# Staggered sets of K pairs with paced loads in an FFN's down product, one Strassen pair more in a convolution's input product, and last output tiles in token halves

## The chip, the cores and the metric

The kernel runs on one core of a Trainium2 chip. The core's TensorE (PE) multiplies, with a separate queue of weight loads (PEld); VectorE (DVE) and ScalarE (ACT) do everything between products; GpSimd (POOL) and SyncE (SP) here only issue transfers, which share 16 DMA engines. Measured is the device time of one execution, in microseconds.

## The reference

A decoder trunk over 1024 tokens of width 1024, in float32:

```
h = x
for i in (0, 1):              # two of each, DEPTH = 2: one convolution layer, one MLA layer
    h = h + short_conv(rms_norm(h), w_in, conv_w, w_out)   or   h + mla(rms_norm(h), ...)
    h = h + swiglu(rms_norm(h), w13, w2)
out = rms_norm(h)

short_conv: u = h @ w_in;  gate_b, gate_c, val = split(u, 3)
            z = gate_c * val;  conv = sum(conv_w[k] * z shifted by 2-k tokens)
            (gate_b * conv) @ w_out
swiglu:     g, u = split(h @ w13, 2);  (silu(g) * u) @ w2        # hidden width 2816
mla:        queries, keys and values from latents, causal softmax per head, then @ w_o
```

The two layers are the convolution layer (loop index 0) and the MLA layer (index 1), each followed by its own FFN.

## The kernel before, in words

**Arithmetic.** Activations are kept transposed: features on the 128 partitions, the 1024 tokens along the free dimension, in two halves T1 and T2 of 512 tokens. An fp32 product is made of three fp32r matmuls: each operand is split (`split`, L90) into a rounded high part (an ACT cast, L92) and a remainder (a DVE subtraction, L93), and high·high, high·low and low·high are accumulated. One matmul is a 128x128 weight block by 512 tokens.

**Two kinds of products.** `classic` (L206) makes two output tiles of 1024 tokens from all K blocks: eight block products per K pair, 96 matmuls for K = 1024. `pair` (L144) is a Strassen–Winograd product of 2x2 blocks (two K blocks by two output tiles by two token halves): seven block products per K pair, "1", "5", "6", "2", "7", "3", "4" in the order `SEQ`, 84 matmuls for K = 1024 (four pairs, so 12 matmuls in a product). Each product needs its own weight mix (DVE additions L155 to L165, then a split into `wo`), and its own token mix, an operand `x1`, `x5`, ... of the K pair. `blocks` (L187) evacuates products 1, 5 and 6 by an ACT copy to half tiles `z` (L194), and the others by a DVE addition. `drip` takes work of other parts (token mixes, gates, statistics) from a queue of closures after each product.

**Stages.** Transposes of x and its split; `conv_in` (`first_product`, L557: the first three output pairs, `CLASSIC = 3`, by `classic`, the others by `blocks`, since the token mixes of x, `mix_x` L570, have to be made first); `conv_out` by `classic` into `h` (L674); FFN 1: `up` (22 output pairs, `blocks`) makes silu(g)·u, the seven operands of each of the 11 pairs of hidden tiles (`operands`, L242) are stored to a DRAM tensor `md` (512 KB each, pair `KEPT = 4` stays on the chip), and `back` (the down product, L475) reads them; the MLA stages with `w_o`; FFN 2 alike; the last norm with transposes back.

**The down product.** `back` runs over `GROUPS` of 2, 3, 3 and 3 K pairs; within a group over four pairs of output tiles `mp`, and for each of them the seven products of that group (6 matmuls in a product with two K pairs, 9 with three), accumulated into `h` by DVE (L500). The operands of a group are 14 or 21 tiles `xm` of 512 KB from a pool of 41 slots; those of the next group are loaded by the POOL queue (`load`, L686, issued in `move`, L85) after each `mp`, `pace` at a time, and the rest after the last `mp`. A load waits until its slot is free. Weights come by SP's queue (L140), four transfers for each `mp`, of 192 KB with three pairs and 128 KB with two, into ten buffers `w`.

**What sets the order.** Each engine's stream is ordered by a scheduler that simulates the program, so the order on an engine is not that of the code alone. Stalls at a place come from the semaphores that the instructions wait for.

## Time and profile before

Median of three runs 2104.06 us (2101.93 to 2107.01). The profiled execution took 2109.98 us, its recorded span is 2108.0 us.

| | before |
|---|---|
| span of the profiled execution | 2108.0 us |
| PE busy | 2071.3 us, 9606 matmuls and transposes |
| DVE busy | 1624.9 us |
| ACT busy | 932.0 us |
| POOL busy (issuing transfers) | 230.5 us |
| bytes moved | 321.24 MB, mean 152 GB/s |
| granted TensorE clock, mean | 0.992 |

Busy times are sums over the span. PE is pipelined, and its ends are modelled: whether PE is fed is better read from the number of matmuls that start in a stretch, at the 227 ns from one start to the next that a fed stretch shows. GB/s is what all queues moved together. "issue to landing" of a transfer includes the time that it stands behind others.

### The profile page before, as it was taken

The page shows a single profiled execution, that of the slowest core. Times are in us where ns is not written, and L with a number is a line of the kernel's source. Part 1 is how long each engine was busy: PE and PEld are TensorE (multiplying, and loading weights), DVE is VectorE, ACT ScalarE, POOL GpSimd, SP SyncE. Part 2 cuts the span into 40 slices and gives each one's busy share as a digit, 9 for nine tenths or more (in the row PEclk, how much of TensorE's full clock was granted, in tenths as well). Part 3 has the DMA queues.
Part 4 walks back from the last instruction along what each step waited for, and adds up shares of the span by engine and source line. Part 5 has one row for each costly group of instructions (what it writes and reads, how often), then busy time and mean ns, then how long its engine had stood idle before and what let it go on. Part 6 is the DMA issues. An engine that isn't in the chain of part 4 may idle for free.

```text
span 2108.0 us, 27158 instructions
## 1 busy us (share of the span) xinstructions
PE 2071.3 (98%) x9606; PEld 1721.6 (82%) x9606; DVE 1624.9 (77%) x2662; ACT 932.0 (44%) x1697; POOL 230.5 (11%) x440
## 2 busy tenths in 40 slices
PE   8999999999999999999999999999999999999998
PEld 6878887888888887788888888887888888878786
DVE  5797757789988887689558877767888888876775
ACT  6633344444444443224445555455444444442235
POOL 1000100000101121110001011100010010121100
PEclk9999999999999999999999999999999999999998
DMA  6133462343544587764222124532454454686751
GB/s 248 35 97 119 141 214 91 120 147 123 185 140 156 174 302 262 258 226 133 85 69 66 38 66 122 178 101 62 140 170 148 133 173 144 216 280 203 268 185 80
DMA packets 263399, 321.24 MB, mean 152 GB/s; under 512 B 18959, under 2 KB 207568, under 8 KB 263264
## 3 DMA queue, kind: packets, MB, share of 16 engines
q0 software_dynamic: 57792, 201.46, 28.0%
q1 hardware_dynamic: 205472, 118.07, 19.0%
q8 instruction: 75, 1.23, 0.2%
q14 instruction: 60, 0.49, 0.1%
HBM read 206.22 MB, written 108.00 MB: 149 GB/s over the span
## 4 chain that ended last, share of the span: by engine, by line
PE 92%; DVE 3%; DMA 2%; ACT 1%; issue 1%; SPq 0%; POOL 0%; POOLq 0%; DVEq 0%; ACTq 0%
PE ps_z L180 37%; PE ps_y L180 27%; PE ps_c L225 7%; PE ps_s L948 4%; PE ps_pv L983 2%; PE ps_t L972 1%; PE ps_wo L105 1%; PE ps_wo L107 1%; PE ps_wo L109 1%; PE ps_l L109 1%; PE ps_l L105 1%; PE ps_l L107 1%; DMA w<-in_mla_ffn_w_dram 1%; PE ps_q L105 1%; PE ps_q L107 1%
## 5 line engine op out<-in xcount | busy, mean ns | idle before, releaser
L180 PE MATMUL ps_z<-x,wo 128*128 128x512 f32 x2532 | 609.9, 390 | 3.6 <-ACT z L194 2.8
L180 PEld LDWEIGHTS ps_z<-x,wo 128*128 128x128 f32 x2532 | 475.5, 188 | 104.7 <-ACT z L194 4.1
L180 PE MATMUL ps_y<-x,wo 128*128 128x512 f32 x1764 | 432.3, 389 | 1.2 <-DVE x L93 0.9
L180 PEld LDWEIGHTS ps_y<-x,wo 128*128 128x128 f32 x1764 | 330.6, 188 | 70.9 <-DVE x L93 1.8
L92 ACT CAST wo<-w 128x512 fp32r<-128x512 f32 (+2 forms) x423 | 238.6, 570 | 281.1 <-PE ps_y L180 110.5
L93 DVE TENSOR_TENSOR wo<-w,wo 128x512 fp32r<-128x512 f32 (+2 forms) x423 | 260.8, 623 | 62.2 <-ACT wo L92 61.4
L180 PE MATMUL ps_z<-xm,wo 128*128 128x512 f32 x960 | 241.9, 395 | 7.9 <-DVE h L500 5.9
L180 PEld LDWEIGHTS ps_z<-xm,wo 128*128 128x128 f32 x960 | 180.8, 190 | 50.5 <-DVE h L500 7.8
L92 ACT CAST wo<-sums 128x512 fp32r<-128x512 f32 (+2 forms) x172 | 98.3, 572 | 260.9 <-PE ps_y L180 101.7
L180 PE MATMUL ps_y<-xm,wo 128*128 128x512 f32 x720 | 182.6, 392 | 2.3 <-DVE h L500 2.3
L180 PEld LDWEIGHTS ps_y<-xm,wo 128*128 128x128 f32 x720 | 135.2, 189 | 31.8 <-DVE h L500 3.1
L85 POOL DMA_DIRECT2D md<-x x140 | 75.0, 536 | 738.1 <-DVE x L93 695.6
L194 ACT COPY z<-ps_z 128x512 f32<-128x512 f32 x106 | 62.0, 585 | 136.5 <-PE ps_z L180 136.4
L93 DVE TENSOR_TENSOR wo<-sums,wo 128x512 fp32r<-128x512 f32 (+2 forms) x172 | 107.4, 624 | 14.2 <-ACT wo L92 12.9
L500 DVE TENSOR_TENSOR h<-ps_z,h 128x512 f32<-128x512 f32 x104 | 71.5, 688 | 40.5 <-PE ps_z L180 39.6
L85 POOL DMA_DIRECT2D xm<-md x140 | 74.1, 536 | 260.1 <-PE ps_z L180 138.3
L93 DVE TENSOR_TENSOR x<-t,x 128x512 fp32r<-128x512 f32 x136 | 92.2, 686 | 5.7 <-ACT x L92 5.7
L234 DVE TENSOR_TENSOR a<-ps_y,z 128x512 f32<-128x512 f32 x88 | 60.7, 689 | 42.3 <-PE ps_y L180 42.1
L92 ACT CAST x<-t 128x512 fp32r<-128x512 f32 x136 | 82.4, 620 | 20.8 <-DVE t L249 20.2
L955 ACT ACTIVATE p<-ps_s,mx,qscale 128x128 f32<-128x128 f32 (+3 forms) x64 | 53.4, 835 | 70.7 <-DVE mx L954 66.7
L155 DVE TENSOR_TENSOR sums<-w,w 128x512 f32<-128x512 f32 (+2 forms) x85 | 53.3, 627 | 31.3 <-DMA w<-in_mla_ffn_w_dram 15.1
L500 DVE TENSOR_TENSOR h<-ps_y,h 128x512 f32<-128x512 f32 x88 | 60.4, 686 | 20.7 <-PE ps_y L180 20.5
(295 smaller groups left out, 3213.6 us busy)
## 6 DMA issues: line engine op xcount, KB each, us to landing
md<-x POOLq DMA_DIRECT2D x140, 512.0 KB, 3.5
xm<-md POOLq DMA_DIRECT2D x140, 512.0 KB, 8.1
w<-in_conv_ffn_w_dram SPq DMA_DIRECT2D x88, 256.0 KB, 2.9
w<-in_mla_ffn_w_dram SPq DMA_DIRECT2D x88, 256.0 KB, 3.0
w<-in_conv_w_in_dram SPq DMA_DIRECT2D x48, 256.0 KB, 3.1
hd<-h POOLq DMA_DIRECT2D x24, 512.0 KB, 3.5
w<-in_conv_ffn_w_dram SPq DMA_DIRECT2D x48, 192.0 KB, 4.7
w<-in_mla_ffn_w_dram SPq DMA_DIRECT2D x48, 192.0 KB, 4.4
```

Of the source, the lines that this page charges most:

```text
L85: nc.gpsimd.dma_start(dst, src)
L92: nc.scalar.copy(out=hi, in_=src)
L93: (eng or nc.vector).tensor_tensor(lo, src, hi.bitcast(F32), ALU.subtract)
L105: nc.tensor.matmul(ps[:, hs], lhsT=wh, rhs=xh(k)[:, hs], start=st, stop=False)
L107: nc.tensor.matmul(ps[:, hs], lhsT=wh, rhs=xl(k)[:, hs], start=False, stop=False)
L180: mm = lambda w_, x_, f: nc.tensor.matmul(b, lhsT=w_[:, m], rhs=x_, start=f, stop=True, skip_group_check=True)
L194: nc.scalar.copy(out=kept[name], in_=b)
L225: nc.tensor.matmul(ps[:, ts], lhsT=w_[:, m], rhs=X[i][f"b{kh}{th}"][:, q, :], start=st and j == 0, stop=en and j == 2)
L234: nc.vector.tensor_tensor(dst, ps, add, ALU.add)
L500: nc.vector.tensor_tensor(dst[name], b, dst[name], ALU.add)
L948: nc.tensor.matmul(ps[:, a:b], lhsT=q[:, qs], rhs=k[:, a:b], start=i == 0, stop=i == 4 and b < kw)
L955: nc.scalar.activation(p, ps[:, :kw], AF.Exp, bias=mx, scale=qscale[:, qb:qb + 1], accum_out=rsum)
```

## The change

1. **conv_in.** `CLASSIC` goes from 3 to 2: the third output pair is made by seven products in place of eight. So that its token mixes are there earlier, `mix_x` and the statistics of x are started behind the first half of the first classic pair (hook `ahead`), and dripped in the numbers of `MIX`. The eight full-width ACT scalings of `xs` (`gains`, L580) go: the mixes take the gain in the DVE operation itself (`scalar_tensor_tensor`), and four half-width ACT scalings are left. The first Strassen pair takes its products in the order `SEQX`, "1", "2", "5", "6", "7", "3", "4", the three that need no mix being 1, 2 and 3. Product 7 of conv_in has its sign turned in both factors.
2. **down.** `GROUPS` becomes `SETS`, eight sets that are used by two `mp` each: `mp` 0 and 1 take (0, 10), (1, 2, 3), (4, 5, 6), (7, 8, 9); `mp` 2 and 3 take (0, 1), (2, 3, 4), (5, 6, 7), (8, 9, 10). A set has two or three pairs, as before, and the number of matmuls is the same. Pair 3 is kept on the chip, pair 10's operands are made first in `up`, and pair 10 is loaded twice: 77 loads in place of 70 for each FFN. A load of `xm` is issued behind the evacuation of a certain product (a dependency that POOL waits for): one load for each 1.5 products for the first 14, then one for 4/3 products. The 14 loads of the first set go one behind each evacuated product of the last two `up` output pairs, what is left of them right after. In the first sets the weight splits are ordered behind the evacuation four products back (`behind`), and the drip is thinner.
3. **conv_out and w_o.** The last output tile is made T2 first, then T1. The operands of the last K pair for the FFN are made in three steps: 1 and 5 before, 6, 3 and 7 behind T2, 2 and 4 behind T1; the statistics of the last four tiles come after that.
4. **Half tiles.** Six shared buffers become three for `z` and three for the rest.

The diff, cut to its core:

```diff
-CLASSIC = 3
+CLASSIC = 2
+MIX = ((3, 4), (5, 4))
-GROUPS = ((0, 1), (2, 3, 4), (5, 6, 7), (8, 9, 10))
-KEPT = 4
+LATE = 4
+SETS = ((0, 10), (0, 1), (1, 2, 3), (2, 3, 4), (4, 5, 6), (5, 6, 7), (7, 8, 9), (8, 9, 10))
+KEPT = 3
+AHEAD = 4
+PACE = (1.5, 10, 4 / 3)
...
     def half(name, dt=F32):
-        return slots.tile([P, HS], dt, name=name, tag="half", bufs=NHALF)
+        kind = "z" if name[0] == "z" else "half"
+        return slots.tile([P, HS], dt, name=name, tag=kind, bufs=NHALF // 2)
...
+    def behind(n):
+        with ExitStack() as stack:
+            seen = set()
+            for inst in reversed(marks[:max(0, len(marks) - n + 1)][-4:]):
+                if inst is not None and inst.ins.engine not in seen:
+                    seen.add(inst.ins.engine)
+                    stack.enter_context(tc.issue_after(inst.ins))
+            yield
...
-            split(hi, lo, source(name))
+            with behind(ahead):
+                split(hi, lo, source(name))
...
-            hook(name, b)
-            drip(1 if len(queue) < 14 else 2)
+            marks.append(hook(name, b))
+            if paced and marks[-1] is not None:
+                paced.popleft()(marks[-1])
+            if name in thin:
+                drip(1 if len(queue) < 14 else 2)
...
+            split_t = late and mi == 2
+            for ths in (((2, T2),), ((1, T1),)) if split_t else (((1, T1), (2, T2)),):
...
+                if split_t:
+                    emit(mi, ps, ths[0][1])
...
-    def back(w, load, st, final, ready, kept):
+    def back(w, load, st, final, ready):
...
+        todo = []
+        for q in range(1, len(SETS)):
+            new = [k for k in SETS[q] if k != KEPT and k not in SETS[q - 1]]
+            todo += [(kp, name) for name in SEQ for kp in new]
+        nload, products = len(todo), [0]
+        def pace(i):
+            return PACE[0] * i if i < 14 else PACE[1] + PACE[2] * i
+        for t in range(2 * len(SETS)):
+            mp, kps = t % (KD // 2), SETS[t // 2]
...
+            def hook(name, b):
...
+                while todo and pace(nload - len(todo)) <= products[0]:
+                    kp, nm = todo.pop(0)
+                    ready.setdefault(kp, {})[nm] = load(kp, nm, done)
+                products[0] += 1
+                return done
...
+            pair(w2, kps, [ready[kp] for kp in kps], n1 * P, n2 * P, hook, thin=("1", "5", "6") if t == 0 else SEQ[::2] if first else SEQ, ahead=AHEAD if first else 99)
...
+        def last(step):
+            mp = KD // 2 - 1
+            n = 2 * mp + (step > 1)
+            if step == 1:
+                fin["x"] = [slot("xg"), slot("xg")]
+                scaled(fin["x"][0], n)
+                X.append({})
+                fin["put"] = operands(*fin["x"], X[mp].__setitem__, "15")
+            else:
+                scaled(fin["x"][1], n, T2 if step == 2 else T1)
+                fin["put"]("637" if step == 2 else "24")
+                drip()
...
+            def ahead(mi):
+                with ExitStack() as behind:
+                    for inst in ready:
+                        behind.enter_context(tc.issue_after(inst.ins))
+                    if run["n"] == 0 and mi == 1:
+                        x_stats()
+                        mix_x()
+                    drip(MIX[run["n"]][mi - 1])
...
-            def mixed(name, x, y, o=o, t=t):
+            def mixed(name, x, g, y, o=o, t=t):
                 t[name] = half("t" + name)
-                tt(t[name], x, t[y] if isinstance(y, str) else y, ALU.subtract)
+                stt(t[name], x, g, t[y], ALU.mult, ALU.subtract)
                 o[name] = op_split("x" + name, t[name])
...
-        def load(kp, name):
+        def load(kp, name, behind=None):
             o = slot("xm", F32R, [P, 2, HS])
-            move(o, md[kp, SEQ.index(name)])
+            d = move(o, md[kp, SEQ.index(name)])
+            if behind is not None:
+                tc.add_manual_dep(d.ins, behind.ins.name, SYNC)
...
-        order = [k for kp in range(KF // 2) if kp != KEPT for k in (2 * kp, 2 * kp + 1)] + [2 * KEPT, 2 * KEPT + 1]
+        kpo = [SETS[0][1]] + [kp for kp in range(KF // 2) if kp not in (KEPT, SETS[0][1])] + [KEPT]
+        order = [k for kp in kpo for k in (2 * kp, 2 * kp + 1)]
...
-            if j == order[-3]:
-                for name in SEQ:
-                    ready[0][name] = load(GROUPS[0][0], name)
-        for name in SEQ:
-            for i, kp in enumerate(GROUPS[0]):
-                if i:
-                    ready[i][name] = load(kp, name)
+            if j in order[-3:-1]:
+                kp = SETS[0][j == order[-2]]
+                for name in SEQ:
+                    paced.append(lambda done, kp=kp, name=name: ready[kp].__setitem__(name, load(kp, name, done)))
```

`project_o` makes its last tile in token halves in the same way as `classic`.

**POOL, end of `up` and start of the down product of FFN 1.** A row is a transfer; brackets hold what it waits for: PE_, DVE_ and Activation_ are those engines' progress, DMASW and DMAHW earlier transfers. Before, the loads of the first group's second pair and of the next group:

```order
L85 DMA md<-x_6136 128x1024 [waits DMASW5_49,DVE_49]
L85 DMA trig<-cos 128x1024 [waits DMASW6_49,Activation_49]
L85 DMA md<-x_6160 128x1024 [waits DMASW7_49,DVE_49]
L85 DMA xm<-md 128x1024 [waits DMASW3_49,DMASW0_49,PE_49]
L85 DMA xm<-md 128x1024 [waits DMASW1_49,PE_49]
L85 DMA xm<-md 128x1024 [waits DMASW2_49,PE_49]
L85 DMA xm<-md 128x1024 [waits DMASW4_49]
L85 DMA xm<-md 128x1024 [waits DMAHW0_49,PE_49]
```

and with the change:

```order
L89 DMA md<-x_6085 128x1024 [waits DMASW2_49,DVE_49]
L89 DMA md<-x_6106 128x1024 [waits DMASW3_49,DVE_49]
L89 DMA xm<-md 128x1024 [waits Activation_49]
L89 DMA xm<-md 128x1024 [waits DMASW6_49,DMASW5_49,Activation_49]
...
L89 DMA md<-x_6142 128x1024 [waits DMASW7_49,DVE_49]
L89 DMA trig<-cos 128x1024 [waits DMASW0_49,Activation_49]
L89 DMA md<-x_6168 128x1024 [waits DMASW1_49,DVE_49]
L89 DMA xm<-md 128x1024 [waits DMASW2_49,DVE_49]
L89 DMA xm<-md 128x1024 [waits DMASW3_49,DVE_49]
```

Before, a load waits for PE, which has to be done with what was in its slot; with the change it waits for the ACT copy or the DVE addition of a product, and the stores to `md` stand between the loads.

**PE, start of conv_in.** `ps_c` is a classic tile, `rp` spreads the statistics, `ps_z` and `ps_y` are Strassen products. Before:

```order
L374 MATMUL vps<-ident,vrows 128x77
L225 MATMUL ps_c<-xb,wc 128x512 x286
L334 MATMUL rp<-identr,rh 128x128
L334 MATMUL rp<-identr,rl 128x128
...
L180 MATMUL ps_z<-xb,wo_839 128x512 x12
L180 MATMUL ps_y<-x_528,wo_858 128x512 x3
L180 MATMUL ps_y<-x_607,wo_858 128x512 x3
```

and with the change:

```order
L252 MATMUL ps_c<-xb,wc 128x512 x142
L364 MATMUL rp<-identr,rh 128x128 x2
L203 MATMUL ps_z<-xb,wo_711 128x512 x12
L364 MATMUL rp<-identr,rl 128x128
...
L203 MATMUL ps_z<-x_406,wo_768 128x512 x2
L252 MATMUL ps_c<-xb,wc 128x512 x48
L203 MATMUL ps_y<-xb,wo_730 128x512 x12
L203 MATMUL ps_z<-x_406,wo_768 128x512
L203 MATMUL ps_z<-x_429,wo_768 128x512 x3
```

The three classic pairs (288 matmuls) are two (192), and product 1 and the start of product 6 of the first Strassen pair stand ahead of the last 48 classic matmuls.

**PE, from conv_out to FFN 1.** `yop` and `yb` are operands of conv_out, `x_...` those of the FFN. Before, behind the last classic matmul:

```order
L225 MATMUL ps_c<-yb_2141,wc 128x512
L180 MATMUL ps_z<-x_2348,wo_2819 128x512 x3
...
L180 MATMUL ps_y<-x_2682,wo_2839 128x512 x3
L180 MATMUL ps_z<-x_2776,wo_2819 128x512
L180 MATMUL ps_y<-x_2781,wo_2839 128x512
...
L180 MATMUL ps_z<-x_2358,wo_2860 128x512 x3
```

and with the change:

```order
L252 MATMUL ps_c<-yop,wc 128x512 x18
L252 MATMUL ps_c<-yb_2142,wc 128x512 x3
L252 MATMUL ps_c<-yb_2145,wc 128x512 x3
L203 MATMUL ps_z<-x_2352,wo_2819 128x512 x3
...
L203 MATMUL ps_y<-x_2690,wo_2839 128x512 x3
L252 MATMUL ps_c<-yop,wc 128x512 x18
L252 MATMUL ps_c<-yb_2136,wc 128x512 x3
L252 MATMUL ps_c<-yb_2139,wc 128x512 x3
L203 MATMUL ps_z<-x_2749,wo_2819 128x512
L203 MATMUL ps_y<-x_2754,wo_2839 128x512
...
L203 MATMUL ps_z<-x_2362,wo_2860 128x512 x3
```

The 18 matmuls of products 1 and 5 with the first three K pairs stand between the two token halves of the last tile, and those with the last K pair follow the T1 half.

254 lines of the change are left out of this document (135 added, 119 removed).

## Prediction

> **What bounds the kernel now.** I read the page first (busy times and the chain of waits by engine), then PE's waits, then the stretches around each wait, then what else ran there.
>
> ```profile
> PE 2071.3 (98%) x9606; PEld 1721.6 (82%) x9606; DVE 1624.9 (77%) x2662; ACT 932.0 (44%) x1697; POOL 230.5 (11%) x440
> PE 92%; DVE 3%; DMA 2%; ACT 1%; issue 1%; SPq 0%; POOL 0%; POOLq 0%; DVEq 0%; ACTq 0%
> 339.79 12.48 PE ps_c L225 x55
> ```
>
> PE is the bound. A piece of the chain without a wait (third row) gives 12.48/55 = 0.227 us for a matmul; this is the price of every matmul below. An edit can gain only by fewer matmuls or by filling PE's gaps, which are few:
>
> ```profile
> PE ps_z L180 <- DVE h L500: 5.9, 2, 3.0
> PE ps_z L180 <- ACT z L194: 2.8, 3, 1.2
> PE ps_y L180 <- DVE h L500: 2.3, 2, 2.0
> PE ps_z L180 <- DVE wo L93: 1.3, 2, 0.8
> PE ps_z L180 <- ACT wo L92: 1.3, 2, 1.1
> PE ps_y L180 <- DVE x L93: 0.9, 2, 0.5
> ```
>
> (Total us, times, longest.) What a gap costs is read from the stretch around it, as its length less its matmuls at 0.227. Columns: length, PE busy, PEld, DVE, ACT, POOL, clock, DMA share, GB/s; the rows are start of down 1, two thirds into its group of pairs 2 to 4, start of down 2, the same place in down 2, conv_out to FFN 1, w_o to FFN 2.
>
> ```profile
> 786.00:796.00 10.00, 8.22 (x33) 5.84 (x33) 8.77 (x20) 5.39 (x13) 1.58 (x3) 1.00 1.13 395
> 868.00:878.00 10.00, 7.11 (x25) 5.40 (x24) 4.30 (x9) 1.48 (x3) 3.10 (x6) 0.83 1.13 395
> 1866.00:1878.00 12.00, 9.76 (x35) 7.27 (x34) 9.86 (x20) 5.42 (x13) 2.64 (x5) 0.86 1.13 391
> 1953.00:1963.00 10.00, 7.02 (x24) 5.35 (x23) 4.64 (x9) 1.54 (x3) 2.96 (x6) 0.83 1.13 394
> 352.00:362.00 10.00, 8.34 (x36) 6.03 (x35) 9.36 (x15) 9.07 (x15) 0.53 (x1) 1.00 0.36 105
> 1435.00:1447.00 12.00, 10.34 (x43) 7.67 (x43) 11.50 (x17) 10.21 (x17) 0.53 (x1) 1.00 0.32 88
> ```
>
> Lost: 10 - 33 x 0.227 = 2.5 us; 4.3; 4.1; 4.6; and from the busy time 1.66 at each of the last two. Single matmul records can be missing, so each is good to some 0.3. The three rows with a clock of 0.83 to 0.86 lose about 1.7 us to it (0.17 x 10): the waits of 2.0 to 3.0 us also halved the clock for a while, which those of up to 1.2 us did not.
>
> The Trainium skill, page "TensorE: Matmul & The Clock Gate", section "Part 1: The HAM clock gate (the "warmup" mystery)", has the clock halve after an idle window of about 3.4 us. Here 2.0 us was enough, so the trace decides. By the page's figure those three places would cost their waits alone, 7.9 us, and the sum below would be -11.8 in place of -16.9.
>
> Why the three are late stands in the chain, and in what POOL did just before:
>
> ```profile
> 863.88 8.48 DMA w<-in_conv_ffn_w_dram
> 1861.50 7.87 DMA w<-in_mla_ffn_w_dram
> 1948.74 8.58 DMA w<-in_mla_ffn_w_dram
> 859.11 1.19 POOL L85 DMA_DIRECT2D xm<-md  x2 [34.24 <-PE ps_z L180]
> 870.66 0.53 POOL L85 DMA_DIRECT2D xm<-md  x1 [0.15 <-issue]
> 873.70 2.49 PE L180 MATMUL ps_z<-xm,wo 128*128 128x512 f32 x6 [2.89 <-DVE h L500]
> xm<-md POOLq DMA_DIRECT2D x140, 512.0 KB, 8.1
> w<-in_conv_ffn_w_dram SPq DMA_DIRECT2D x88, 256.0 KB, 2.9
> w<-in_conv_ffn_w_dram SPq DMA_DIRECT2D x48, 192.0 KB, 4.7
> ```
>
> POOL waits 34 us for slots and then issues 12 loads between the fourth and fifth of these rows: 12 x 524 KB at the 395 GB/s of the window row are 16 us of transfers. A weight load of 192 KB that falls among them takes 8.48 us, where 256 KB in `up` take 2.9. The DVE sum that needs the weights stands ahead of the DVE addition to `h` that PE waits for. Without the 2.89 us the load could have taken 5.6.
>
> **The change part by part.** Durations are from the one profiled execution (2109.98 us, span 2108.0); it is 5.9 us above the median of the runs, 2104.06, and I apply the sum to the median.
>
> *Down, steady.* The matmuls are the same. Seven loads more for each FFN are 14 x 0.53 us of POOL issue and 14 x 1.3 us of transfer (524 KB at 395 GB/s); POOL is 11% busy, so neither lies on PE's path. What matters is the pace. With three pairs a product is 9 x 0.227 = 2.04 us, a load for 4/3 products is 193 GB/s, and the weights (4 x 197 KB for seven products) 55: 248. With two pairs, 1.36 us and 1.5 products: 257 + 55 = 312. Both are below 395, and a weight load finds at most one or two `xm` loads ahead of it: 2.9 us (as in `up`) and 1.3 for one give 4.2, under 5.6. In the changed order a load of `xm` stands 64 and more matmuls (14.5 us) ahead of its first use, after the first set, against a landing of 8.1. So I take the three stalls as gone: -(4.3 + 4.1 + 4.6) = -13.0. Bounds: 0 (all stay) and -13.0. If a load gets late after all, its product is what PE waits for, at a price like those three rows, 4.3.
>
> *Down, start.* The two-pair products are short for DVE:
>
> ```profile
> L93 DVE TENSOR_TENSOR wo<-w,wo 128x256 fp32r<-128x256 f32 x18 | 7.3, 420 | 4.7 <-ACT wo L92 4.7
> L500 DVE TENSOR_TENSOR h<-ps_z,h 128x512 f32<-128x512 f32 x46 | 31.6, 688 | 16.3 <-PE ps_z L180 15.8
> L93 DVE TENSOR_TENSOR x<-t,x 128x512 fp32r<-128x512 f32 x4 | 2.7, 686 | 0.0
> 778.55 9.70 DMA xm<-md
> ```
>
> A product of 1.36 us asks 0.42 of split, up to 0.42 of weight sum and 0.69 of accumulation, 1.1 to 1.5, while the operands of the last hidden pair (0.69 of split, and a mix and a cast) are still in the queue: hence DVE's 8.77 of 10 in the first window row, and 2.5 us lost. The change drips these operands at fewer products and sets the splits four evacuations back, but the DVE work is the same. I take half, -1.2; bounds 0 and -2.5. At the seam the loads are closer than elsewhere: the order has the tightest 38 matmuls (8.6 us) ahead of its use, and eight loads, two stores and `trig` within 62 matmuls (14.1 us): 5.8 MB, 409 GB/s against the 395 seen, 0.5 us over. POOL waits at each paced load for a product; behind it stand stores of the last pair to `md`, whose slots nobody needs within those 14 us. At the nearest rows a late load costs between 0.5 and 4.3 for each FFN; I take nothing, as half of the gap at the start is left in the sum.
>
> *conv_in.* One pair has 12 matmuls fewer: -2.7. The waits at the first Strassen pair, and the work that moves forward:
>
> ```profile
> 118.22 2.56 PE L180 MATMUL ps_z<-x,wo 128*128 128x512 f32 x10 [0.83 <-DVE wo L93]
> 123.48 2.79 PE L180 MATMUL ps_z<-x,wo 128*128 128x512 f32 x11 [0.44 <-ACT z L194]
> 24.50:90.20 65.70, 65.70 (x284) 54.27 (x285) 35.92 (x63) 42.95 (x112) 0.53 (x1) 0.98 0.26 88
> L580 ACT ACTIVATE xs<-xs,vec x8: 1157/1160/1166, 25.8 to 40.7; 128x1024 f32<-128x1024 f32 x8
> L406 ACT ACTIVATE sq<-xt 128x256 f32<-128x256 f32 x32 | 12.8, 412 | 0.0
> L92 ACT CAST x<-t 128x512 fp32r<-128x512 f32 x16 | 8.8, 632 | 0.0
> L93 DVE TENSOR_TENSOR x<-t,x 128x512 fp32r<-128x512 f32 x16 | 10.5, 686 | 2.0 <-ACT x L92 2.0
> ```
>
> The cover shrinks from 284 classic matmuls (65.7 us) to 192 (43.6). ACT had 42.95 in the longer stretch; it loses 8 x 1.16 and gains four half-width scalings (0.63 each, as a cast), so 36 us have to go into 43.6, with DVE's mixes (16 x (0.69 + 0.69) = 22) behind them in turn. Walking the changed order with these durations I find ACT late by about 1.5 us where product 6 waits for its cast and the next classic tile for its copies, and by 0.6 us at product 5: 2.1 in place of today's 0.83 + 0.44 = 1.3. Net -2.7 + 0.8 = -1.9. Bounds: -4.0 (no wait left), and +1.9 if these waits merge into one that halves the clock (4.6, as in the fourth window row).
>
> *conv_out and w_o.*
>
> ```profile
> 354.61 3.73 ACT x L92 x7
> 357.90 0.73 PE L180 MATMUL ps_y<-x,wo 128*128 128x512 f32 x2 [0.47 <-DVE x L93]
> 359.82 2.56 PE L180 MATMUL ps_z<-x,wo 128*128 128x512 f32 x10 [1.19 <-ACT z L194]
> ```
>
> Today the last tile's seven casts fill ACT, and the `z` copy that product 6 needs stands behind them. With halves, x1 and x5 are ready behind the T1 matmuls, so 0.47 goes; the `z` copies then stand behind the T1 scaling (0.63, as a cast of this width) and a square, and I expect two waits of some 0.6 us: 1.2 in place of 1.66 at each of the two, -0.4 each, -0.8 together. Bounds 0 and -3.3. The half pool gives `z` three buffers for three tiles at a time, and moves nothing.
>
> Sum: -13.0 - 1.2 - 1.9 - 0.8 = -16.9. The profiled execution would be 2093.1, the median 2087.2. As runs shorter than the profiled one may have shorter late loads to win back, I round up: **2088**.
>
> **Rivals.**
>
> *The loads collide at the seam.* Against it speaks 409 to 395 GB/s, a small excess; for it, that DVE is full there (8.77 of 10), so a late load finds no slack. If each start of down keeps or makes a stall of 4.3 us, 2 x 4.3 = 8.6 come back: 2096.
>
> The Trainium skill, page "DMA: Bandwidth & Descriptors", section "Specifications", gives about 358 GB/s as the limit of HBM for a core; by that the 14.1 us at the seam would be 16.1, which is this rival. The trace has 395 GB/s over 10 us, so I give the page's figure little weight.
>
> *Nothing is gained beyond conv_in.* Twelve loads in a row are gone, but DVE does the same work in down (77% busy over the span), and a mean pace of 312 GB/s with bunching in POOL's queue could make 4 us stalls elsewhere. Three stalls of 4.3 us that only change place leave -1.9 - 0.8 = -2.7 or, with conv_in at its worse bound, about +1: 2101 to 2105, around 2102.
>
> *Slower: paced loads late in the two-pair sets.* If a load takes the 9.70 us of the start of down rather than 8.6, each of seven products waits 1.1 us, and as its evacuation releases the next load, the lateness is handed on. With the clock halved meanwhile (7 x 1.36 more), 7.7 + 9.5 = 17.2 for each FFN, 34 for both, against -16.9: 2121. It decides from a landing of 8.6 us on, at one load for each product. Against it: 9.70 was measured among some ten loads in a row, and only three of the loads have less than 11 us.
>
> **How the numbers follow.** Forecast (2080 to 2095) 0.62; seam 0.16; no gain 0.13; slower 0.09. Low end: all bounds together, -13.0 - 2.5 - 4.0 - 3.3 = -22.8, would be 2081; with a run's spread, 2080. High end: the seam with a poor conv_in, 2101. A measurement here can tell about 0.2%, 4.2 us, from no change: faster than 2099.9 has 0.62 + 0.16, within it 0.13, slower 0.09.
>
> **What would show it.** In the changed profile, the chain has no weight load of 8 us in the down products, and no stretch of 10 us there has a clock below 0.95; PE's waits for DVE `h` fall from 8.2 us to under 2; the loads of `xm` land in under 8.1 us, spread evenly; conv_in has a wait of 1 to 2 us around 60 to 65 us, and the start of FFN 1 one of about 0.6 twice. Wrong would be: a wait for `xm` in the first set; a halved clock in conv_in; weight loads of 192 KB still at 4.7 us.

## The result, and the profile after

The change took 2114.14 us (median of six runs, 2107.26 to 2116.11) against 2106.65 us for the kernel before (six runs, 2101.93 to 2109.38). The ratio is 1.0039, 95% interval 1.0027 to 1.0052: slower, by more than a measurement can tell from no change, and above the upper end of the range. The profiled execution of the change took 2113.69 us, its span 2111.9, 3.9 us above the span before. The profiled execution of the kernel before (2109.98 us) is slower than any of its six runs here, so the two profiles show about half of the 7.5 us between the medians.

From the page of the changed kernel, busy times of the engines and two kinds of transfers (size, median us from issue to landing):

```profile
PE 2069.0 (98%) x9594; PEld 1719.5 (81%) x9594; DVE 1629.7 (77%) x2674; ACT 927.9 (44%) x1698; POOL 237.6 (11%) x454
xm<-md POOLq DMA_DIRECT2D x154, 512.0 KB, 5.1
w<-in_conv_ffn_w_dram SPq DMA_DIRECT2D x48, 192.0 KB, 4.2
```

The 12 matmuls are gone, and the loads of `xm` land in 5.1 us where they took 8.1. The weight loads of `down` are at 4.2 us in the median where they were at 4.7. By medians the change did what it says. PE's waits of the changed kernel (total us, times, longest) say something else:

```profile
PE ps_z L203 <- DVE h L533: 16.9, 9, 4.0
PE ps_z L203 <- ACT z L220: 1.4, 2, 0.8
PE ps_c L252 <- ACT v L265: 0.8, 1, 0.8
```

L533 is the old L500, the addition of a product to `h`; before, PE waited for it four times, 8.2 us in all. Now it does so nine times, and no row of the view names `xm`. The chain of waits of the changed kernel (start, length, what) has behind these stalls weight loads, and loads of `hs`, the residual, which `back` adds to `h` in the third quarter of `down` (L549, the old L513):

```profile
873.44 7.18 DMA w<-in_conv_ffn_w_dram
889.60 6.52 DMA w<-in_conv_ffn_w_dram
...
937.05 7.65 DMA hs<-hd
...
946.68 3.80 PE ps_z L203 x9
...
955.80 7.72 DMA w<-in_conv_ffn_w_dram
```

The loads are no longer than the worst of before (8.48 and 8.58 us), but there are more of them that somebody waits for. After the stall the nine matmuls at 946.68 take 3.80 us, 0.42 each: the halved clock again. What is late at 873.44 is seen on DVE. From the timeline of DVE in the changed kernel (start, busy, instruction, in brackets the idle time before it and its releaser):

```profile
872.86 0.55 DVE L99 TENSOR_TENSOR wo<-w,wo 128x384 fp32r<-128x384 f32 x1
...
876.63 1.02 DVE L99 TENSOR_TENSOR wo<-w,wo 128x384 fp32r<-128x384 f32 x2
880.74 0.56 DVE L176 TENSOR_TENSOR sums<-w,w 128x384 f32<-128x384 f32 x1 [3.10 <-DMA w<-in_conv_ffn_w_dram]
881.22 0.68 DVE L533 TENSOR_TENSOR h<-ps_z,h 128x512 f32<-128x512 f32 x1
```

The split at 872.86 frees a buffer, and the weight load starts at 873.44 (the chain). DVE comes to the sum that reads these weights (L176) at 880.74 - 3.10 = 877.64, 4.2 us behind the start of the load, and waits 3.10 us for the rest of its 7.18. The addition L533, for which PE waits, comes behind this sum in DVE's stream and is held up with it. PE then stands for 1.59 us:

```profile
881.96 3.92 PE L203 MATMUL ps_z<-xm,wo 128*128 128x512 f32 x16 [1.59 <-DVE h L533]
```

Nobody needs this sum soon: it belongs to the pair of output tiles after next, some 22 us further on. The kernel before has such a sum at the same place:

```profile
872.48 0.56 DVE L155 TENSOR_TENSOR sums<-w,w 128x384 f32<-128x384 f32 x1 [4.39 <-DMA w<-in_conv_ffn_w_dram]
```

DVE came to it at 872.48 - 4.39 = 868.09, also 4.2 us behind the start of its load (863.88, of 8.48 us). So this distance is not new.

The waits view groups DVE's waits for transfers in `down` of FFN 1 (785 to 1000 us), first of before, then of the change:

```profile
DVE sums L155 <- DMA w<-in_conv_ffn_w_dram: 9.6, 6, 4.4
DVE h L513 <- DMA hs<-hd: 0.5, 1, 0.5
```

```profile
DVE sums L176 <- DMA w<-in_conv_ffn_w_dram: 10.6, 4, 4.2
DVE h L549 <- DMA hs<-hd: 7.8, 5, 5.2
```

The waits for weights are about the same; those for `hs` are new. The tile view of `hs` has the eight loads and the eight additions of this FFN (durations in ns, first and last start in us), first before, then the change:

```profile
L512 SPq DMA_DIRECT2D hs<-hd x8: 338/339/362, 876.2 to 931.6; - x8
L513 DVE TENSOR_TENSOR h<-h,hs x8: 1218/1220/1227, 897.4 to 944.3; 128x1024 f32<-128x1024 f32 x8
```

```profile
L548 SPq DMA_DIRECT2D hs<-hd x8: 339/366/436, 890.1 to 937.5; - x8
L549 DVE TENSOR_TENSOR h<-h,hs x8: 1217/1226/1226, 898.2 to 947.4; 128x1024 f32<-128x1024 f32 x8
```

Load by load, DVE came to these additions 4.9 to 30.3 us behind the start of the load before, and 2.6 to 9.4 us with the change. The loads took 3.7 to 12.2 us before and 5.0 to 9.8 with the change: they are not slower, their readers are closer.

What this costs PE is seen over the same 215 us (length, busy times with counts, clock, DMA share, GB/s; matmuls are counted in the first bracket), first before, then the change:

```profile
785.00:1000.00 215.00, 210.12 (x911) 171.28 (x910) 169.48 (x297) 72.27 (x137) 28.55 (x54) 0.99 0.68 225
```

```profile
785.00:1000.00 215.00, 202.41 (x867) 163.89 (x866) 160.99 (x283) 71.11 (x137) 34.45 (x66) 0.98 0.76 236
```

At 0.227 us a matmul that is 8.2 us lost before and 18.2 with the change. The table below does the same sum by parts of the program for each profiled execution: over all matmuls, the time from one start to the next beyond what a fed stretch shows, in us. Its first columns answer to the parts of the prediction; "seams" are conv_out to FFN 1 and w_o to FFN 2. `down` ends with its last matmul; the waits of the last norm are under "other". Each part is good to some tenths, `up` comes out slightly below nothing, and each row is one execution of its kernel. The experiments in it follow below.

```
                           conv_in  seams  up 1+2  down 1  down 2  other  total
before                         1.5    5.0    -0.6     8.7    10.9   22.9   48.4
the change                     2.1    2.9    -0.5    18.1     9.1   23.3   54.9
change, old down               2.1    3.0     8.2     8.3    11.1   23.7   56.2
before, new down               1.5    4.9    -0.5    17.4    10.0   23.7   57.1
change, all splits 4 back      2.1    2.8    -0.6     4.5     2.2   23.7   34.8
before, splits 4 back          1.5    6.6    -0.5    10.5     9.7   24.1   51.7
change, splits 12 back         2.1    2.9    -0.6     9.6     9.0   25.0   47.9
change, 4 back, not paced      2.1    2.8    -0.6     4.9     1.3   23.2   33.7
change, old down, 4 back       3.0    3.0     6.2    11.3     9.0   22.0   54.5
change, loads not paced        2.9    2.8    -0.6     6.9     8.7   21.3   42.0
before, new down, 4 back       1.5    6.5    -0.6     5.9     2.5   21.6   37.5
change, 12 back, hs too        2.1    2.9    -0.6     4.9     3.7   23.7   36.6
change, hs ordered             2.1    2.8    -0.6     8.3    13.3   24.0   49.8
change, few xm loads           2.1    2.9    -0.7     1.8     1.9   22.8   30.8
```

Between the first two rows lies 54.9 - 48.4 = 6.5, and with 12 matmuls fewer (2.7) 3.8 us, the 3.9 us between the spans. Nearly all of the loss is in `down`, 27.2 in place of 19.6, and there in that of FFN 1 (18.1 for 8.7), while that of FFN 2 lost 1.8 less. There the additions of `hs` wait 0.7 us in all, in FFN 1 7.8.

### The profile page after: what moved, and what is told of

Its sections match the earlier page's. It is cut to its first block, busy times and chain, and to the rows that moved or that the text cites. A ratio compares the mean times of both kernels' runs of the same rounds, so it can differ in the third digit from the quotient of the medians.

```text
span 2111.9 us, 27202 instructions
## 1 busy us (share of the span) xinstructions
PE 2069.0 (98%) x9594; PEld 1719.5 (81%) x9594; DVE 1629.7 (77%) x2674; ACT 927.9 (44%) x1698; POOL 237.6 (11%) x454
## 4 chain that ended last, share of the span: by engine, by line
PE 88%; DVE 5%; DMA 4%; issue 2%; ACT 1%; POOL 0%; SPq 0%; POOLq 0%; DVEq 0%; ACTq 0%
PE ps_z L203 35%; PE ps_y L203 26%; PE ps_c L252 6%; PE ps_s L1019 4%; PE ps_pv L1054 2%; PE ps_t L1043 1%; DMA w<-in_conv_ffn_w_dram 1%; PE ps_wo L112 1%; PE ps_wo L114 1%; PE ps_wo L116 1%; DMA w<-in_mla_ffn_w_dram 1%; PE ps_l L116 1%; PE ps_l L112 1%; PE ps_l L114 1%; DVE h L533 1%
## 5 line engine op out<-in xcount | busy, mean ns | idle before, releaser
L203 PE MATMUL ps_z<-x,wo 128*128 128x512 f32 x2568 | 616.8, 389 | 1.7 <-ACT z L220 1.4
L203 PEld LDWEIGHTS ps_z<-x,wo 128*128 128x128 f32 x2568 | 481.6, 188 | 103.5 <-ACT z L220 3.2
L203 PE MATMUL ps_z<-xm,wo 128*128 128x512 f32 x960 | 245.9, 398 | 17.7 <-DVE h L533 16.9
L203 PEld LDWEIGHTS ps_z<-xm,wo 128*128 128x128 f32 x960 | 181.6, 191 | 62.6 <-DVE h L533 18.2
L89 POOL DMA_DIRECT2D xm<-md x154 | 81.5, 531 | 377.3 <-DVE h L533 256.9
L533 DVE TENSOR_TENSOR h<-ps_z,h 128x512 f32<-128x512 f32 x104 | 71.3, 688 | 42.6 <-PE ps_z L203 42.5
L176 DVE TENSOR_TENSOR sums<-w,w 128x512 f32<-128x512 f32 (+2 forms) x86 | 54.0, 628 | 53.3 <-DMA w<-in_conv_ffn_w_dram 21.7
L533 DVE TENSOR_TENSOR h<-ps_y,h 128x512 f32<-128x512 f32 x88 | 60.4, 688 | 16.9 <-PE ps_y L203 16.5
```

The costliest lines, as they stand in the source:

```text
L89: return nc.gpsimd.dma_start(dst, src)
L176: tt(sums, R["12"], R["22"], ALU.add)
L203: mm = lambda w_, x_, f: nc.tensor.matmul(b, lhsT=w_[:, m], rhs=x_, start=f, stop=True, skip_group_check=True)
L533: done = nc.vector.tensor_tensor(dst[name], b, dst[name], ALU.add)
```

## The experiments

The theory, called A where an expectation letters it: the change is slow because additions on DVE stand a few us behind the start of the load that they read, while the spread `xm` traffic makes most weight and `hs` loads longer than that; what blocks DVE blocks the evacuation, and PE. Its rivals: the other parts of the change (conv_in, the halves) cost the time; or the extra and spread traffic is simply too much in itself, whatever stands where; or POOL's waits for evacuations cause it, or the pace they set. Ratios are to the kernel before, run beside each.

**Which part it is.** Two kernels take the change apart. The first is the changed kernel with the old order of `down` (groups of 2, 3, 3, 3 and their block loads), everything else new:

```diff
-SETS = ((0, 10), (0, 1), (1, 2, 3), (2, 3, 4), (4, 5, 6), (5, 6, 7), (7, 8, 9), (8, 9, 10))
-KEPT = 3
+GROUPS = ((0, 1), (2, 3, 4), (5, 6, 7), (8, 9, 10))
+KEPT = 4
...
-    def back(w, load, st, final, ready):
+    def back(w, load, st, final, ready, kept):
...
```

> The changed kernel with the down product of before (groups, loads in blocks, pair 4 kept), so that conv_in, conv_out, w_o and the half tiles are the only changes. From the two profiles these are worth -1.9 us in conv_in (12 matmuls fewer, 0.7 us more waits) and -1.0 and -1.1 us at the two seams. Theory 1 (the loss is all in down): 4 us under before, some 2102 to 2103. Rival (the loss comes from the earlier parts as well): 2106 or more.

2115.1 us, ratio 1.0042 (1.0027 to 1.0056). A miss by 12 us, in the range of the rival. The other is the kernel before with the new `down` alone (three classic pairs and whole last tiles, as before):

```diff
-GROUPS = ((0, 1), (2, 3, 4), (5, 6, 7), (8, 9, 10))
-KEPT = 4
+SETS = ((0, 10), (0, 1), (1, 2, 3), (2, 3, 4), (4, 5, 6), (5, 6, 7), (7, 8, 9), (8, 9, 10))
+KEPT = 3
+AHEAD = 4
+PACE = (1.5, 10, 4 / 3)
...
-    def back(w, load, st, final, ready, kept):
+    def back(w, load, st, final, ready):
...
```

> The kernel before with only the down product of the change (staggered sets, paced loads, pair 3 kept). Theory 1: the down products lose 27 us to stalls in place of 19, so 8 us over before, some 2114 to 2115, with stalls late in each down product. Rival (the parts hurt one another, for instance through buffers shared with conv_out): within 4 us of before.

2116.43 us, ratio 1.0048 (1.0031 to 1.0065), as expected: `down` alone makes the kernel slower, 27.4 us lost there in the table where the old order lost 19.6. So the loss does not need conv_in or the halves. But the first kernel shows that the parts do not add up. Its `down` loses what it lost before (19.4), and new stalls appear in `up`, where neither kernel had any. Its chain:

```profile
1808.84 10.97 DMA w<-in_mla_ffn_w_dram
...
1821.28 3.65 PE ps_z L203 x9
```

This is the block of seven `xm` loads at the end of `up`. Before, the sum at the end of `up` waited 0.55 us; here, given another program and so another order from the scheduler, the sum stands so that it waits 7.1 us of such a load, and PE pays with a stall and the slow clock (nine matmuls in 3.65 us). The same mechanism, in another place.

**Move the additions, leave the traffic.** In the first sets the changed kernel orders each weight split, with the sum that feeds it, behind the evacuation four products back (`AHEAD`). The next kernel does this in all sets, one token of difference:

```diff
-            pair(w2, kps, [ready[kp] for kp in kps], n1 * P, n2 * P, hook, thin=("1", "5", "6") if t == 0 else SEQ[::2] if first else SEQ, ahead=AHEAD if first else 99)
+            pair(w2, kps, [ready[kp] for kp in kps], n1 * P, n2 * P, hook, thin=("1", "5", "6") if t == 0 else SEQ[::2] if first else SEQ, ahead=AHEAD)
```

> The changed kernel with one difference: the weight sums and splits are ordered behind the evacuation four products back in all sets, not in the first only. In the built order the DVE sum of a set's weights then stands 20.9 us behind what releases its load, in place of 3.6 us. Theory A (a DVE sum that stands right behind its weight load holds up the evacuations behind it, and the steady loads of xm make that load slower than its 4 to 6 us): the stalls behind weight loads go in both down products, 12 to 16 us less than the change, 2098 to 2102; those behind the loads of hs in the first down product stay. Theory B (only the additions of hs do it): 2112 to 2114. Theory C (the traffic of the paced loads itself, or the seven loads more): no change, 2114.

2094.0 us, ratio 0.9946 (0.9931 to 0.9961): 20 us below the change, 4 below the expected range, and faster than before. The expectation's 20.9 and 3.6 us are of the built order. In the trace, DVE comes to the sums of most later sets 20.3 us behind the start of their load, and came to those that waited in the change 2.6 to 4.2 us behind it. The additions of `hs` also moved, to 12.0 to 14.7 us behind their loads (2.6 to 9.4 in the change), which had not been expected. The loads are hardly different. The tile view of `w` between 860 and 985 us, last row, of the change and then of this kernel:

```profile
DMA to landing us min/median/max: 2.5/4.6/11.3
```

```profile
DMA to landing us min/median/max: 2.5/5.3/7.4
```

A median of 5.3 us costs nothing where 4.6 us cost stalls, and the longest, 7.4, is still as long as the loads that stalled the change. The sum of this kernel in the same stretch shows no wait on the timeline, and PE works from 844.91 to 879.9 without one (the first and the last two of 16 pieces of its chain, all of them PE):

```profile
869.36 0.55 DVE L176 TENSOR_TENSOR sums<-w,w 128x384 f32<-128x384 f32 x1
```

```profile
844.91 0.91 PE ps_z L203 x4
...
876.42 2.04 PE ps_z L203 x9
878.46 1.59 PE ps_y L203 x7
```

The rivals by which the extra traffic or POOL's waits are too much in themselves fall here: both are as in the change. What this run does not tell is the weight sums from the additions of `hs`, since both moved. First, this kernel with the `hs` additions queued one output pair later:

```diff
+            queue.extend(later)
+            later = []
...
-                    queue.append(lambda m=m, x=x: nc.vector.tensor_tensor(st[m], st[m], x, ALU.add))
+                    later.append(lambda m=m, x=x: nc.vector.tensor_tensor(st[m], st[m], x, ALU.add))
```

> As the one before, and the additions of hs (the stored residual) are queued one pair of output tiles later than their loads are issued. Theory A with B: all stalls late in the down products go, some 22 us less than the change, 2091 to 2094. Theory A alone: as the one before. Theory C: 2114.

2093.39 us, ratio 0.9943 (0.9928 to 0.9958), the same as without it: the edit did not move the additions against their loads (12.0 to 14.7 us again), and at this distance none had waited. Then the changed kernel with a smaller dose, the splits 12 evacuations back:

```diff
-            pair(w2, kps, [ready[kp] for kp in kps], n1 * P, n2 * P, hook, thin=("1", "5", "6") if t == 0 else SEQ[::2] if first else SEQ, ahead=AHEAD if first else 99)
+            pair(w2, kps, [ready[kp] for kp in kps], n1 * P, n2 * P, hook, thin=("1", "5", "6") if t == 0 else SEQ[::2] if first else SEQ, ahead=AHEAD if first else 12)
```

> The changed kernel with the weight sums and splits of the later sets ordered behind the evacuation twelve products back in place of four: the first weight sum then stands 7.7 us behind what releases its load, against 3.6 us in the change and 20.9 us in the kernel with four. The weight loads of the change took 2.5 to 8.5 us. Theory A: nearly all of the gain, 2094 to 2099. Rival D (what helps is that splits come close to their product and leave DVE to the evacuations, not the time that a load has): little of it, 2106 or more.

2106.82 us, ratio 1.0012 (0.9999 to 1.0024). Better than the change, but some 8 us above the expectation of the theory and in the range of rival D. The sums now stand 7.1 us behind their loads in the trace (7.7 in the built order) and hardly wait; what is left are two stalls of 5 us, both behind `hs`. PE's waits and the chain of this kernel:

```profile
PE ps_z L203 <- DVE h L533: 9.5, 2, 5.0
```

```profile
934.70 7.74 DMA hs<-hd
...
942.53 1.23 DVE h L549
...
944.42 4.21 PE ps_z L203 x9
```

To take these away the additions were queued one pair later (the edit to `queue` and `later` above), with the splits 12 back:

> The kernel with the weight sums behind twelve products (7.7 us from release to sum) and the additions of hs one pair later. That kernel without the second edit took 2106.8 and its profile has one stall of 5.4 and one of 4.9 us, each with a halved clock behind it, both behind loads of hs and none behind a weight load. Theory A with B: both go, 2106.8 - 5.4 - 4.9 - 2 x 1.7 = 2093. Theory A without B: 2106.

2105.61 us, ratio 0.9996 (0.9983 to 1.0008), a miss by 12 us. And the same edit in the change itself, splits as they are there:

> The changed kernel with one difference: the additions of hs are queued one pair of output tiles later than their loads are issued, and the weight sums stay where the change has them (3.6 us behind what releases their loads). Theory A with B: of the 27 us that the change loses in down, those behind hs go (7.8 us of DVE waits in the first down product, of which some 5 reach PE with the clock), the stalls behind weight loads stay: 2106 to 2110. If the additions of hs are the whole cause: 2095. If they do nothing: 2114.

2109.44 us, ratio 1.0016 (1.0003 to 1.003). It lies where it was expected, but says little: queueing an addition later in the program did not move it on DVE against its load. In both runs DVE still came to the additions 2.1 to 9.5 us behind the start of their loads. In the first of the two it waited even longer for `hs` than the 11.5 us without the edit (tile view of `hs`, 850 to 990 us: total, times):

```profile
  DMA hs<-hd: 13.8, 5
```

So the addition has to be ordered, as the splits are:

```diff
+                    def plus(m=m, x=x):
+                        with behind(4):
+                            nc.vector.tensor_tensor(st[m], st[m], x, ALU.add)
-                    queue.append(lambda m=m, x=x: nc.vector.tensor_tensor(st[m], st[m], x, ALU.add))
+                    later.append(plus)
```

With the splits 12 back:

> Weight sums behind twelve products (7.7 us from release to sum), and each addition of hs ordered behind the evacuation four products back, one pair of output tiles later: in the built order it stands 7.7 to 16.8 us behind what releases its load, in place of 4.1 to 8.2 (the loads took 5 to 10 us). If the additions of hs are the same cause as the weight sums: the stalls of 5 to 6 us, with the halved clock behind them, go: 2093 to 2097. If not: 2104 to 2107, as without it.

2095.86 us, ratio 0.9956 (0.9941 to 0.9971), as expected; nothing in `down` of FFN 1 waits for `hs` any more. The splits are 12 back as in the run of 2106.82, so rival D, by which their place against the product decides, falls here. And in the change, weight sums left where they are:

> The changed kernel with the same ordering of the additions of hs, and the weight sums where the change has them (3.6 us). If both are the same cause, and each holds a part: the stalls behind weight loads stay, two or three of 2 to 5 us in each down product: 2103 to 2110. If hs alone is the cause: 2095. If the weight sums alone are: 2114.

2105.69 us, ratio 0.9997 (0.9984 to 1.0009), as expected; the ten runs lie between 2096.95 and 2108.41, and the profiled one is the slowest. DVE's waits in `down` of FFN 1 now hold the weights alone:

```profile
DVE sums L176 <- DMA w<-in_conv_ffn_w_dram: 6.7, 5, 2.8
```

Each of the two kinds of additions holds a part of the loss: with either one alone moved (0.9997 and 1.0012), the time is that of before, with both moved 0.9946 to 0.9956. Against the kernel before, the slowdown is thus of the size of the part of `hs` alone (8.4 us, from 2114.14 to 2105.69); the stalls at the weights are those that were there before and that were to go.

**Take the traffic, leave the weight sums.** The changed kernel with most loads of `xm` in `down` left out; the products read pairs 1, 2 and 3 again in place of 4 to 10, so its time is that of a program that moves less, while every product, sum and weight load stays:

```diff
-            new = [k for k in SETS[q] if k != KEPT and k not in SETS[q - 1]]
+            new = [k for k in SETS[q] if k in (1, 2) and k not in SETS[q - 1]]
...
+        same = {0: 0, 1: 1, 2: 2, 3: 3, 4: 1, 5: 2, 6: 3, 7: 1, 8: 2, 9: 3, 10: 1}
-            pair(w2, kps, [ready[kp] for kp in kps], n1 * P, n2 * P, hook, thin=("1", "5", "6") if t == 0 else SEQ[::2] if first else SEQ, ahead=AHEAD if first else 99)
+            pair(w2, kps, [ready[same[kp] if t >= 4 else kp] for kp in kps], n1 * P, n2 * P, hook, thin=("1", "5", "6") if t == 0 else SEQ[::2] if first else SEQ, ahead=AHEAD if first else 99)
```

> The changed kernel with most loads of xm in the down products left out: from the third pair of output tiles on, products use the operands of pairs 1, 2 and 3 again in place of those of pairs 4 to 10, so that 14 loads are issued there in place of 63. The first weight sums stand 3.6 to 10 us behind what releases their loads. Theory A: weight loads take about 2.6 us, no sum waits for one, and the down products lose 8 to 12 us in place of 27: 2095 to 2100. If the order alone makes the stalls, traffic or not: 2110.

2089.15 us, ratio 0.9925 (0.9911 to 0.994), below the expected 2095 to 2100. The tile view of `w` and the 215 us of `down` 1:

```profile
DMA to landing us min/median/max: 2.5/2.5/3.5
```

```profile
785.00:1000.00 215.00, 214.62 (x940) 175.76 (x939) 176.20 (x308) 78.30 (x150) 9.55 (x18) 1.00 0.42 133
```

So a weight load is late by the traffic beside it: 2.5 us in the median and 3.5 at most here, 4.6 and 11.3 in the change. The sums kept their places (DVE comes to one at 877.5 us, 4.3 behind the start of its load at 873.2), and none of them waits. For the weight sums the loss thus needs both, a late load and an addition right behind it. For `hs` this run does not tell, since it moved these too. The view of `hs` (as above) has their loads some 80 us earlier than the change, 86 to 121 us ahead of the additions:

```profile
L549 SPq DMA_DIRECT2D hs<-hd x8: 338/466/1163, 801.1 to 812.8; - x8
L550 DVE TENSOR_TENSOR h<-h,hs x8: 1218/1220/1222, 887.4 to 934.0; 128x1024 f32<-128x1024 f32 x8
```

**Is it POOL's wait, or the pace?** The kernel with all splits four back, its `xm` loads no longer waiting for an evacuation, only for their slot:

```diff
-                    ready.setdefault(kp, {})[nm] = load(kp, nm, done)
+                    ready.setdefault(kp, {})[nm] = load(kp, nm)
```

> The kernel with the weight sums behind four products in all sets, but the loads of xm in the down product no longer wait for the evacuation of a product: they go as soon as a slot is free and POOL comes to them. Theory A: the pace does not matter once the sums stand far behind the loads, 2092 to 2097. Rival (it takes both, the pace and the order): loads bunch and stalls return, 2100 or more.

2091.6 us (2090.43 to 2092.94), ratio 0.994 (0.9925 to 0.9955). This is the lowest time of a version that does the whole work, just under the expected range; by the intervals it cannot be told from the paced 2094.0. Its weight loads are the worst of the fast kernels (view of `w`, then its PE waits):

```profile
DMA to landing us min/median/max: 2.5/6.0/14.9
```

```profile
PE ps_z L203 <- ACT wo L98: 1.9, 2, 1.7
```

These long loads cost PE one wait of 1.7 us, behind one of 13.67 in the chain. With the additions well behind (`hs` by 11.1 us and more), the pacing is not needed. The same edit in the change itself, sums right behind their loads (the same line of the diff):

> The changed kernel with the order of its weight sums, but the loads of xm in the down product do not wait for the evacuation of a product. Theory A: up to eight loads of xm are outstanding in place of four, weight loads get slower (up to 15 us), and the sums stand 3.6 to 11 us behind their release: at least as slow as the change, 2112 to 2125. Rival (the wait for an evacuation is itself what costs: DVE is late, the loads bunch): under 2106.

2102.74 us, ratio 0.9981 (0.9971 to 0.9992). A miss: I had expected no gain, and the time lies in the range of the rival. The last 35 us of `down` 1 in the change, and then in this kernel (before has x155 there too), show part of why:

```profile
940.00:975.00 35.00, 27.19 (x105) 21.55 (x105) 22.01 (x35) 9.61 (x16) 4.22 (x8) 0.90 0.73 229
```

```profile
940.00:975.00 35.00, 35.00 (x155) 28.77 (x155) 31.61 (x52) 15.19 (x23) 3.23 (x6) 1.00 0.48 150
```

Loads that do not wait for their turn are done early: POOL issues its last but two at 928.26 here (the last at 930.55 before), but goes on to 966.83 in the change. Without `xm` loads beside them, the last sets lose nothing. But the edit moved a second thing: the first `hs` load starts at 868.3 here (890.1 in the change), DVE comes to these additions 14.4 to 24.5 us behind their loads, and none waits. Ordering `hs` alone had taken the change from 2114.14 to 2105.69. So most of the 11 us may be the place of `hs` again, and that spreading the loads is a cost in itself is not shown.

**Is the order enough by itself?** The splits four back in the kernel before, loads in blocks as they were:

```diff
-            split(hi, lo, source(name))
+            with behind(ahead):
+                split(hi, lo, source(name))
...
-                pair(w2, g, ready, n1 * P, n2 * P, hook)
+                pair(w2, g, ready, n1 * P, n2 * P, hook, ahead=4)
```

> The kernel before with one difference: in the down product the weight sums and splits are ordered behind the evacuation four products back, so that a set's first weight sum stands some 20 us behind what releases its load (3.6 to 11.8 us before). Groups, loads in blocks and everything else as before. Theory A (a DVE sum close behind its weight load holds up the evacuations): the stalls behind weight loads go although the loads of xm still come in blocks and slow the weight loads to 8 to 11 us; the down products lose some 10 us in place of 19.6, so about 2096. Rival (the blocks of loads are the cause, and only pacing or staggering them helps): 2103 to 2106.

2113.64 us, ratio 1.0045 (1.003 to 1.006), and the same order in the changed kernel with the old `down`, the first of these experiments:

```diff
-                pair(w2, g, ready, n1 * P, n2 * P, hook)
+                pair(w2, g, ready, n1 * P, n2 * P, hook, ahead=AHEAD)
```

> The changed kernel with the down product of before and with its weight sums ordered behind the evacuation four products back. The run with the old down product alone took 2115 us and lost 8.2 us in the two up products (at the block of seven loads near their ends, in weight loads of 11 us) and 19.4 in the down products. Theory A: the stalls of down go to some 10 us, those of up stay, since the order is changed in down only: about 2106. If the staggered sets are worth something of their own in down, this kernel loses more there than the changed one with the same order (10 us).

2114.5 us, ratio 1.0047 (1.003 to 1.0063). Both missed, by 18 and 8 us. Neither kernel lost less in `down` than before (20.2 and 20.3 us in the table, 19.6 before); where the first lost the rest of its 9.5 us, the table shows only in part. The chain of the first shows two weight loads in 21 us, and the tile views of `w` (868 to 878 us) and then of `xm` (860 to 880 us) how long they and their neighbours took:

```profile
873.50 21.36 DMA w<-in_conv_ffn_w_dram x2
```

```profile
DMA to landing us min/median/max: 12.6/17.2/18.1
```

```profile
DMA to landing us min/median/max: 3.7/10.2/14.5
```

POOL issues 17 `xm` loads between 861 and 879, and a weight load in that block takes 12.6 to 18.1 us. Here the lead was too short: DVE came to one sum 15.8 us behind the start of a load of 18.0, and PE waited 5.2 us in all for casts of weights. Whether a still longer lead would do was not tried. With the staggered sets the longest weight load of that stretch is 7.4 us paced and 14.9 not paced, both under the lead of 20. The last kernel joins the two: the kernel before with the new `down` alone (as above), splits four back everywhere, old conv_in and last tiles.

```diff
-            pair(w2, kps, [ready[kp] for kp in kps], n1 * P, n2 * P, hook, thin=("1", "5", "6") if t == 0 else SEQ[::2] if first else SEQ, ahead=AHEAD if first else 99)
+            pair(w2, kps, [ready[kp] for kp in kps], n1 * P, n2 * P, hook, thin=("1", "5", "6") if t == 0 else SEQ[::2] if first else SEQ, ahead=AHEAD)
```

> The kernel before with the down product of the change and the weight sums behind four products in all sets; conv_in, conv_out, w_o and the half tiles as before. Against the kernel with all parts and the same order (2094.0) it lacks conv_in (profiles: -1.9) and the two seams (-1.0 and -1.1). Theory 1: 2098. If those parts are worth nothing: 2094.

2098.4 us, ratio 0.9966 (0.9954 to 0.9979), as expected. This one line is worth some 17 us on the new `down` (0.82% between the two ratios), and conv_in with the halves the rest to 0.9946, 4.2 us, of which the intervals (0.9954 to 0.9979 and 0.9931 to 0.9961) leave the size open.

## Why the prediction was wrong, by its steps

*What bounds the kernel.* Right: PE's time is its matmuls and a few gaps, and the sums of gaps account for the 3.9 us between the two spans to 0.1 us.

*Down, steady, -13.0.* Wrong, and it is the step that failed: "a weight load finds at most one or two `xm` loads ahead of it", 4.2 us, "under 5.6", so "the three stalls as gone". The 4.2 us is what the median load of 192 KB in FFN 1 took, to the tenth; but the stalls come from the longest, and those of FFN 1 shown above took 6.5 to 7.7 us. The room of 5.6 us, a load less PE's wait for it, held at two of them (7.18 less 1.59, and 6.52 less 0.92) and had shrunk to 3.9 at the last (7.72 less 3.85): a distance that the scheduler sets anew in every program was taken for a constant. The term left out altogether, put at nothing without a word, is `hs`: its additions came 4.9 to 30.3 us behind their loads before and waited 0.5 us in FFN 1, and with the change 2.6 to 9.4 us behind and waited 7.8. One of the three stalls, at the start of the second `down`, did go. In all, `down` behind the first sets (the first four pairs of output tiles) lost 24.1 us where it had lost 11.1: +13.0, where -8.9 (4.3 and 4.6) stood. That a gain of the forecast size was there the runs confirm: with the additions moved, `down` loses 6.7 in both FFNs together, 12.9 below before, where -13.0 and -1.2 stood.

*Down, start, -1.2.* The first sets lost 1.6 and 1.5 us in place of 3.4 and 5.0, which is -5.4 where -5.3 stood (the -1.2, and the 4.1 of the stall at the second start). In these sets the change itself orders the splits four back. The loads did not collide at the seam; no wait for `xm` is on PE's list.

*conv_in, -1.9.* 12 matmuls fewer are -2.7, and the gaps grew from 1.5 to 2.1: -2.1. Right in both parts (1.3 and 2.1 were forecast).

*conv_out and w_o, -0.8.* -1.0 and -1.1 us, -2.1 together: mis-sized, at less than half of what it was. One wait of 0.7 us is left at conv_out and none at w_o, where I expected two of 0.6 at each place.

*The rivals.* The sign came out as in the one called slower, at 0.09, but not by its mechanism: it had loads of `xm` late in the two-pair sets, and these land in 5.1 us with nobody waiting. Nearest in mechanism is "nothing is gained beyond conv_in", stalls of some 4 us that change place; it had as many of them as before, and there are more. (Its own terms take the high end of the seam rival to 2099.8, not 2101.) The right one was within reach of the numbers. A sum on DVE that waits for a weight load was quoted as the cause of the old stalls; what I did not ask is how many other loads have an addition as close behind them, and which of these would meet traffic once it was spread. Of the signs named ahead, the landing of `xm` came true, no weight load reached 8 us in the chain, and the weight loads were at 4.2, not "still at 4.7": signs by median and by size said nothing. The two that failed are those of waiting: PE's waits for DVE `h` rose to 16.9 us where under 2 was named, and the clock fell to 0.90 over the 35 us from 940.

## What to carry to other kernels

Where an engine works in order, an instruction that reads a load delays all that is queued behind it; so compare, for each load, the distance from its start to its first reader with the longest landing beside other traffic, not with the median. Ordering the readers well behind their loads (weights 20.3 us in place of 2.6 to 4.2, `hs` 12 and more in place of 2.6 to 9.4) was worth 20 us of 2114 here, and then loads of up to 14.9 us did little harm; at 18 us they did again. A place that a scheduler chose is no constant: when any part of the program changes, work out the distances again from the new order. This holds for an experiment too: two of those above moved the `hs` loads without being meant to.

## What the runs showed of the hardware

How much a small weight load suffers from large ones was not expected: 192 KB take 2.5 us with hardly any other traffic, 2.5 to 8.5 with paced `xm` loads of 512 KB in flight (twice 11.3, beside two `hs` loads), and 12.6 to 18.1 inside a block of 17, while those 512 KB loads themselves land in 5.1 us (paced) and 10.2 (in the block), by medians. In the block, the load with less than half of the bytes takes longer than the large one. Why was not tried.

Whether a wait of PE also halves its clock does not follow from its length alone. In the change, waits of 3.96, 3.85 and 1.80 us are each followed by 3.41 us at half the clock, and one of 2.30 us (at 2049.79) is not. At w_o to FFN 2, waits of 0.5 and 1.2 us left the clock of the kernel before at 1.00 and halved it for 3.41 us with the splits four back. So the 1.7 us that the prediction adds to a stall is what three stalls cost, not a rule.
